# Remainders of two plain weight blocks per slab in the first MLP product: a negative on ScalarE and an adding transfer from GpSimd's queue instead of a subtraction on VectorE

## The chip, the cores and the metric

The kernel runs on one core of a Trainium2 chip. The metric is the device time of one execution in microseconds (us), the median of several runs. One more execution is recorded by the hardware profiler; all durations of single instructions come from that one.

Five engines have instruction streams of their own and meet through semaphores: TensorE (PE; its weight loads are listed as PEld), VectorE (DVE), ScalarE (ACT), GpSimd (POOL) and SyncE (SP). Nearly all transfers are issued by SP. A transfer that adds to its destination is issued here by GpSimd.

## The reference

One decoder block on an input of 2048 rows by 1024 channels: a norm, a combined input projection, two mixers (a short gated convolution and a gated linear recurrence), an output projection with a residual, and then the MLP that this change is in:

```python
h = rmsnorm(x, norm_mlp_g[l])
z = jnp.square(jax.nn.relu(jnp.einsum('bsd,df->bsf', h, w_mlp_in[l])))
x = x + jnp.einsum('bsf,fd->bsd', z, w_mlp_out[l])
return rmsnorm(x, final_norm_g)
```

`w_mlp_in` is 1024 by 4096 in float32. It is called `w1` in the kernel.

## The kernel before

The rows are worked in two pairs of blocks of 512 rows. Each pair runs through mixers, output projection and MLP, so the MLP comes twice. In the profiled execution its first product runs at about 468 to 775 us for the first pair and at about 1485 to 1792 us for the second; its second product (`Down`) follows each time.

**Three passes.** TensorE multiplies operands of type fp32r, a rounded float32. Each float32 operand is split in two: `hi` is its rounded copy, `lo` the remainder. Each product is then three passes, `w_hi*H_hi`, `w_hi*H_lo`, `w_lo*H_hi`, and in the code they come in that order for each quarter of the contraction: the third matmul of a product is the first that reads `w_lo`. The split is `split_into` (its two operations are lines 181 and 182): a copy on ScalarE, then a subtraction on VectorE. `split_new` takes two new tiles for it.

**Slabs and products.** The first product is made in eight slabs of 512 columns of `w1`, one object of the class `Up` each (s = 0 to 7). A slab's weights are four raw blocks of 128 x 1024 elements (512 KB): a11, a12, a21, a22, loaded by SP. A scheme with seven products in place of eight works on them. Two products take a raw block as it came from memory (product 1 takes a11, product 2 takes a12). The others take sums made on VectorE by `sums` (s3, s2, and in place a21 and, at line 833, a12), and product 4 takes a22. `prepare(i)` (lines 835 to 837 with the split) makes the two halves for product i. `multiply` (line 857) issues its 24 matmuls. `drain` takes the results from PSUM (copies `snap` at line 869, a relu and a square at lines 874 and 875, sums at lines 886 to 914) and stores them as `d_z`.

**Order.** The products of a slab come as 1, 2, 6, 5, 7, 3, 4. Slabs 0, 1, 2 do their products 1 and 2 first, then their other five; slabs 3 to 7 follow one after the other. `prepare` is called two products ahead of its `multiply` (`LEAD1 = 2`), `sums` four ahead (`SUMS1 = 4`):

```python
for n in range(-LEAD1, len(seq)):
    m = n + LEAD1
    if prepared <= m < len(seq):
        ups[seq[m][0]].prepare(seq[m][1])
    m = n + SUMS1
    if 0 <= m < len(seq):
        ups[seq[m][0]].sums(seq[m][1])
```

In the first pair's MLP, TensorE keeps the order of the code, and a scheduler puts the instructions of ScalarE, VectorE, GpSimd and SP in order. Between the MLP's own instructions it places those that prepare weights for later stages (the `sum_hi` rows on ScalarE). At the start of the second pair's MLP (`pair_before_mlp`, with the last transposes of the block's rows, line 1742), VectorE's and ScalarE's orders are written out too, and slab 0's products 1 and 2 and slab 1's product 1 are prepared there.

GpSimd does next to nothing: 71 operations in the whole kernel, one transfer among them (the gains `gm`, line 2095). It has no instruction in the two stretches of the first product.

Of the kernel before, what the change touches and what calls it, by code (L numbers as in the profile page):

```python
# [10 lines left out]
F32R = mybir.dt.float32r  # L11
AF = mybir.ActivationFunctionType
ALU = mybir.AluOpType
MUL, ADD, SUB, MAX = ALU.mult, ALU.add, ALU.subtract, ALU.max
# [50 lines left out]
def block_kernel(  # L65
# [15 lines left out]
    nc = tc.nc  # L81
# [30 lines left out]
    def wtile(name, shape, dt=F32):  # L112
        return wp.tile(list(shape), dt, tag="w", name=name)
# [66 lines left out]
    def split_into(hi, lo, src, lo_engine=None):  # L180
        nc.scalar.copy(hi, src)  # L181
        return (lo_engine or V).tensor_tensor(lo, src, hi.bitcast(F32), SUB).ins  # L182
# [32 lines left out]
    def take(nm, ahead=AHEAD, lo_engine=None):  # L215
        u = cursor[0]
        assert units[u][0] == nm, (units[u][0], nm)
        cursor[0] += 1
        for v in range(u + 1, u + ahead + 1):
            load_unit(v)  # L220
        if ahead and not (u + ahead + 1 < len(units) and is_kept(u + ahead + 1)):
            load_unit(u + ahead + 1)
        for v in range(u + 1, u + ahead + 1):
            if v < len(units) and units[v][0] == "oB1":
                with tc.high_priority(SOONER):
                    split_unit(v, lo_engine)
            else:
                split_unit(v, lo_engine)
        if KEEP(u, NU):
            put_by(u, splits[u])  # L230
        return splits.pop(u)
# [249 lines left out]
    with tc.manual_schedule(  # L481
# [9 lines left out]
        w = (his, los)  # L491
# [36 lines left out]
        w = take("g0", ahead=0)  # L528
# [9 lines left out]
        w = take("x1", ahead=0)  # L538
# [254 lines left out]
    def split_new(src, new, nm, lo_engine=None):  # L793
        shape = list(src.shape)
        hi = new(nm + "_hi", shape, F32R)
        lo = new(nm + "_lo", shape, F32R)
        made_at["split"] = split_into(hi, lo, src, lo_engine)
        return hi, lo

    class Up:  # L800


# [6 lines left out]
        def load(self, fs=range(2)):  # L809
            v = w1[:, 512 * self.s : 512 * self.s + 512].rearrange(  # L810
                "(h k p) (f c) -> f h p k c", p=P, h=2, f=2
            )
            for f in fs:
                pair = []
                for h in range(2):
                    r = wtile("w1", (P, 4, 256))
                    nc.sync.dma_start(r, v[f, h])
                    pair.append(r)
                if f == 0:
                    self.a11, self.a12 = pair  # L820
                else:
                    self.a21, self.a22 = pair
# [11 lines left out]

        def prepare(self, i):
            src = {1: "a11", 2: "a12", 6: "s2", 5: "a21", 7: "s3", 3: "a12", 4: "a22"}[i]
            self.ready[i] = split_new(getattr(self, src), wtile, "w")

        def multiply(self, i, H):
            w = self.ready.pop(i)  # L840
# [466 lines left out]
    def prepare_sums():  # L1307
# [23 lines left out]
        for nm in PORDER:  # L1331
            a11, a21, a22 = load(nm, 0, 0), load(nm, 1, 0), load(nm, 1, 1)
            yield
            yield
            s3 = temp("s3", W)
            tt(s3, a11, a21, SUB)
            tt(a21, a21, a22, ADD)
            yield
            a12 = load(nm, 0, 1)
            tt(a11, a21, a11, SUB)  # L1340
            hi = split(s3)
            yield
            put(nm, 7, hi, s3)
            hi = split(a21)
            yield
            put(nm, 5, hi, a21)
            tt(a12, a12, a11, SUB)
            yield
            hi = split(a11)
            yield  # L1350
            put(nm, 6, hi, a11)
            hi = split(a12)
            yield
            put(nm, 3, hi, a12)
            yield
# [4 lines left out]
    def prepare_out_sums():  # L1360
# [25 lines left out]
        for g in range(3):  # L1386
            b12, b11, b22 = load(g, 0, 1), load(g, 0, 0), load(g, 1, 1)
            yield
            yield
            t3 = temp("t3", W)  # L1390
            tt(t3, b22, b12, SUB)
            tt(b12, b12, b11, SUB)
            yield
            b21 = load(g, 1, 0)
            tt(b22, b22, b12, SUB)
            hi = split(t3)
            yield
            put(7, g, hi, t3)
            hi = split(b12)
            yield  # L1400
            put(5, g, hi, b12)
            tt(b21, b21, b22, SUB)
            hi = split(b22)
            yield
            put(6, g, hi, b22)
            hi = split(b21)
            yield
            put(4, g, hi, b21)
# [510 lines left out]
    def pair_before_mlp(b, ups):  # L1919
# [165 lines left out]
        def in_sixth(n, t):  # L2085
            prepare(5, s1, n)
            if n < 3:
                fourth_sum(n)
# [28 lines left out]
        def in_fifth(n, t):  # L2117
            prepare(3, of(0, 1), n)
            square(b, t, 0, True)
# [3 lines left out]
        def in_third(n, t):  # L2123
            prepare(7, of(1, 0), n)
            square(b, t, 1, False)
            scaled(b, t, root(b, t))
            if n == 3:
                raw0.extend(temp("raw0") for _ in range(4))
                turn(xs[TORDER[0]], TORDER[0], raw0, gm)
# [299 lines left out]
```

## Time and profile before

| what | value |
| --- | --- |
| median of 3 runs | 2106.95 us (2106.58 to 2107.22) |
| the profiled execution | 2106.28 us, of which 2104.5 us is the span from the first to the last instruction |
| granted TensorE clock in it | 0.999 of full speed |
| first product, first pair | about 468 to 775 us of the span |
| first product, second pair | about 1485 to 1792 us of the span |
| the split's cast and subtraction of one block | 1.05 us on ScalarE, 1.22 us on VectorE |

In a row of the timeline the first number is the start in us of the span, the second how long the row lasts, then engine, line, operation, output tile, input tiles and their shapes; `x3` joins three instructions that follow each other, and brackets at the end tell how long the engine stood idle before and who released it. In the chain of waits the numbers are start and length of a stretch. A table by stretches of time gives, for each stretch, the busy time of PE, PEld, DVE, ACT and POOL, then the granted clock, the mean busy share of the DMA engines, and GB/s.

### The profile page before, as it was taken

The numbers are of one execution on the slowest core, as the hardware profiler recorded it, in microseconds if no ns is written. First come the engines' busy times: TensorE is split into PE (matmuls) and PEld (weight loads), VectorE is DVE, ScalarE is ACT, GpSimd is POOL, SyncE is SP. The second block draws the span as 40 slices with busy tenths as digits, with TensorE's granted clock in tenths as the row PEclk, the third lists the DMA queues.
The fourth block names the chain that finished last, engine by engine and source line by source line (L and its number), as shares of the span: only waits on it lengthen the run. The fifth ranks groups of instructions, "written<-read, shape, count | busy, mean of one in ns | idle before, by whom it ended". The sixth has DMA issues, their size and how long they took to land.

```text
span 2104.5 us, 25165 instructions
## 1 busy us (share of the span) xinstructions
PE 2096.0 (100%) x9396; PEld 1726.4 (82%) x9396; DVE 1603.7 (76%) x1848; ACT 1104.2 (52%) x1438; POOL 54.8 (3%) x71
## 2 busy tenths in 40 slices
PE   9999999999999999999999999999999999999998
PEld 7888888888888888888888887888888888888887
DVE  6889538858775777999997876785886765887776
ACT  6875447726554554444455888234764333333344
POOL 0110000000000000000000100000000000000000
PEclk9999999999999999999999999999999999999999
DMA  9988889743667778689564656775343355854432
GB/s 340 333 307 326 316 327 352 283 174 111 239 251 255 274 286 333 236 315 338 210 259 169 216 207 230 266 266 208 121 166 134 145 185 208 310 178 155 140 120 81
DMA packets 204762, 492.98 MB, mean 234 GB/s; under 512 B 15840, under 2 KB 80352, under 8 KB 204640
## 3 DMA queue, kind: packets, MB, share of 16 engines
q1 hardware_dynamic: 203040, 486.65, 63.9%
q10 hardware_dynamic: 1568, 4.72, 0.6%
q8 instruction: 74, 1.21, 0.2%
q14 instruction: 48, 0.39, 0.1%
q0 software_dynamic: 32, 0.00, 0.0%
HBM read 324.59 MB, written 166.72 MB: 233 GB/s over the span
## 4 chain that ended last, share of the span: by engine, by line
PE 99%; DVE 1%; ACT 0%; issue 0%; POOL 0%; ACTq 0%; POOLq 0%
PE up L857 42%; PE dn L975 28%; PE po L267 6%; PE ps_g L240 4%; PE wo_x L1889 3%; PE ps_x L240 3%; PE ps_v L240 2%; PE ps_b L240 2%; PE ps_c L240 2%; PE wo_w L1889 2%; PE wo_y L1889 1%; PE tps L1742 1%; PE psri L1498 1%; PE psri L692 1%; PE start_x L518 1%; PE start_x L240 1%
## 5 line engine op out<-in xcount | busy, mean ns | idle before, releaser
L857 PE MATMUL up<-H,w_hi 128*128 128x512 f32 x2576 | 795.0, 390 | 0.0
L857 PEld LDWEIGHTS up<-H,w_hi 128*128 128x128 f32 x2576 | 482.3, 188 | 102.5 <-issue 1.8
L857 PE MATMUL up<-H,w_lo 128*128 128x512 f32 x1288 | 501.5, 389 | 0.0
L975 PE MATMUL dn<-w_hi,z_hi 128*128 128x512 f32 x864 | 336.1, 389 | 0.0
L975 PE MATMUL dn<-w_lo,z_hi 128*128 128x512 f32 x864 | 336.1, 389 | 0.0
L975 PE MATMUL dn<-w_hi,z_lo 128*128 128x512 f32 x864 | 336.1, 389 | 0.0
L857 PEld LDWEIGHTS up<-H,w_lo 128*128 128x128 f32 x1288 | 241.7, 188 | 51.4 <-DVE w_lo L182 0.9
L181 ACT CAST z_hi<-z 128x1024 fp32r<-128x1024 f32 x112 | 118.0, 1053 | 306.3 <-PE dn L975 213.7
L182 DVE TENSOR_TENSOR w_lo<-w,w_hi 128x1024 fp32r<-128x1024 f32 x156 | 190.4, 1222 | 68.1 <-ACT w_hi L181 25.8
L181 ACT CAST w_hi<-w 128x1024 fp32r<-128x1024 f32 x156 | 162.5, 1049 | 131.4 <-PE up L857 52.6
L975 PEld LDWEIGHTS dn<-w_lo,z_hi 128*128 128x128 f32 x864 | 162.2, 188 | 33.9
L975 PEld LDWEIGHTS dn<-w_hi,z_lo 128*128 128x128 f32 x864 | 162.2, 188 | 33.7
L975 PEld LDWEIGHTS dn<-w_hi,z_hi 128*128 128x128 f32 x864 | 162.2, 188 | 33.4
L1007 DVE TENSOR_TENSOR x<-dn,x 128x1024 f32<-128x1024 f32 x108 | 131.1, 1222 | 23.2 <-PE dn L975 23.0
L182 DVE TENSOR_TENSOR z_lo<-z,z_hi 128x1024 fp32r<-128x1024 f32 x112 | 136.7, 1220 | 3.0 <-ACT z_hi L181 3.0
L869 ACT COPY snap<-up 128x1024 f32<-128x1024 f32 x48 | 48.7, 1015 | 73.9 <-PE up L857 73.4
L874 ACT ACTIVATE snap<-snap 128x1024 f32<-128x1024 f32 x33 | 35.1, 1062 | 75.7 <-DVE snap L894 26.5
L182 DVE TENSOR_TENSOR w_lo<-raw,w_hi 128x1024 fp32r<-128x1024 f32 x44 | 53.3, 1221 | 12.1 <-ACT w_hi L181 9.7
L1889 PE MATMUL wo_x<-w_o,y_hi 128*128 128x512 f32 x192 | 59.8, 392 | 0.0
L267 PE MATMUL po<-w_hi,y_hi 128*128 128x512 f32 x192 | 59.6, 393 | 0.0
L267 PE MATMUL po<-w_hi,y_lo 128*128 128x512 f32 x192 | 59.4, 390 | 0.0
L267 PE MATMUL po<-w_lo,y_hi 128*128 128x512 f32 x192 | 59.2, 389 | 0.0
(425 smaller groups left out, 3290.1 us busy)
## 6 DMA issues: line engine op xcount, KB each, us to landing
z<-d_z SPq DMA_DIRECT2D x112, 512.0 KB, 5.9
w<-in_w_mlp_in_dram SPq DMA_DIRECT2D x64, 512.0 KB, 5.9
d_z<-snap SPq DMA_DIRECT2D x64, 512.0 KB, 3.3
w_hi<-d_w SPq DMA_DIRECT2D x55, 512.0 KB, 6.4
w_lo<-d_w SPq DMA_DIRECT2D x55, 512.0 KB, 6.1
d_z<-z SPq DMA_DIRECT2D x48, 512.0 KB, 3.0
w<-in_w_mlp_out_dram SPq DMA_DIRECT2D x48, 512.0 KB, 8.8
d_w<-w_hi SPq DMA_DIRECT2D x40, 512.0 KB, 6.6
```

Source lines behind the costliest of these rows:

```text
L181: nc.scalar.copy(hi, src)
L182: return (lo_engine or V).tensor_tensor(lo, src, hi.bitcast(F32), SUB).ins
L240: nc.tensor.matmul(ps[:, j, lo:hi], ws[k // 4][:, k % 4, j * P : (j + 1) * P], hs[:, k, lo:hi], start=k == 0 and i == 0, stop=k == KD - 1 ...
L267: nc.tensor.matmul(ps[:, half, :], ys[:, j, t * P : (t + 1) * P], ws[j][:, 0, half * 512 : (half + 1) * 512], start=first and i == 0, stop ...
L518: nc.tensor.matmul(start_x[:, j], w[a][k // 4][:, k % 4, j * P : (j + 1) * P], h[c][:, k], start=k == 0 and n == 0, stop=k == KD - 1 and n ...
L692: nc.tensor.matmul(pr_[:, e, :], ws[own, c - gates[2], :], xsrc[own, j, :], start=i == 0, stop=i == 2)
L857: nc.tensor.matmul(ps[:, j, :], ws[:, k, j * P : (j + 1) * P], hs(k), start=i in (1, 2, 5) and k == 0 and n == 0, stop=k == 3 and n == len ...
L869: made_at["snap"] = nc.scalar.copy(t, ps).ins
L874: nc.scalar.activation(t, t, AF.Relu)
L975: nc.tensor.matmul(ps[t // 2][:, t % 2, :], zs[:, p, t * P : (t + 1) * P], ws[:, p, :], start=i in (1, 2, 5) and a == 0 and p == 0 and n == 0,
L1007: V.tensor_add(xt[b, th, dh], ps[th], xt[b, th, dh])
L1889: nc.tensor.matmul(ps[t // 2][:, t % 2, :], ys[:, j, t * P : (t + 1) * P], ws[:, j, :], start=first and n == 1, stop=final and n == 6 * le ...
```

## The change

For products 1 and 2 of slabs 1 to 7 (14 blocks in each of the two MLPs, 28 in all), `lo` is no longer made by VectorE. ScalarE writes the rounded copy `hi` as before, and right behind it a second operation writes the negative of the raw block, rounded in the same way, into `lo`. Then a transfer issued from GpSimd's queue adds the raw block to `lo`, in place: `lo = -round(src) + src`. For product 1 the transfer reads the raw block from memory a second time (`self.raw`, 128 partitions with four runs of 1 KB each); for product 2 it reads the tile a12 (128 runs of 4 KB). Slab 0 and all other products keep the subtraction.

```diff
+    def split_by_queue(src, again, new, nm):
+
+        shape = list(src.shape)
+        hi = new(nm + "_hi", shape, F32R)
+        lo = new(nm + "_lo", shape, F32R)
+        nc.scalar.copy(hi, src)
+        nc.scalar.activation(lo, src, AF.Copy, scale=-1.0)
+        nc.gpsimd.dma_start(lo, again, accum_op=ADD)
+        return hi, lo
+
...
+            self.raw = v[0, 0]
...
         def prepare(self, i):
             src = {1: "a11", 2: "a12", 6: "s2", 5: "a21", 7: "s3", 3: "a12", 4: "a22"}[i]
-            self.ready[i] = split_new(getattr(self, src), wtile, "w")
+            src = getattr(self, src)
+            if i in (1, 2) and self.s > 0:
+                again = self.raw if i == 1 else src
+                self.ready[i] = split_by_queue(src, again, wtile, "w")
+            else:
+                self.ready[i] = split_new(src, wtile, "w")
```

The lines behind it shift by 10 and then by 16: the matmul of line 857 is line 873 after, the copies and relus of lines 869, 874 and 875 are 885, 890 and 891. The new cast is line 805, the negative line 806, the adding transfer line 807.

The next rows show ScalarE before slab 5 of the first pair, as the kernel before has them: the last three rows of slab 4's work, then the casts for slab 4's product 4 (`w_hi_5379`) and for slab 5's products 1 and 2 (`w_hi_5412`, `w_hi_5458`).

```order
L874 ACTIVATE snap_5363<-snap_5363 128x1024
L875 ACTIVATE snap_5363<-snap_5363 128x1024
L181 CAST w_hi_5379<-w1_5094 128x1024
L181 CAST w_hi_5412<-w1_5371 128x1024
L181 CAST w_hi_5458<-w1_5373 128x1024
L874 ACTIVATE snap_5328<-snap_5328 128x1024
L875 ACTIVATE snap_5328<-snap_5328 128x1024
```

The same place after the change, where `w_lo_5421` and `w_lo_5468` are the remainders of slab 5's products 1 and 2.

```order
L890 ACTIVATE snap_5371<-snap_5371 128x1024
L891 ACTIVATE snap_5371<-snap_5371 128x1024
L181 CAST w_hi_5387<-w1_5100 128x1024
L805 CAST w_hi_5420<-w1_5379 128x1024
L806 ACTIVATE w_lo_5421<-w1_5379 128x1024
L805 CAST w_hi_5467<-w1_5381 128x1024
L806 ACTIVATE w_lo_5468<-w1_5381 128x1024
L890 ACTIVATE snap_5336<-snap_5336 128x1024
L891 ACTIVATE snap_5336<-snap_5336 128x1024
```

The casts keep their place; each negative stands directly behind its cast, and the second cast moves back by one operation.

ScalarE before slab 3 of the first pair is another case. After the change it reads as follows (`w_lo_4864` is the remainder of slab 3's product 1).

```order
L181 CAST w_hi_4823<-w1_4506 128x1024
L805 CAST w_hi_4863<-w1_4815 128x1024
L890 ACTIVATE snap_4810<-snap_4810 128x1024
L806 ACTIVATE w_lo_4864<-w1_4815 128x1024
L891 ACTIVATE snap_4810<-snap_4810 128x1024
```

Here the relu of a result tile stands between the cast and its negative.

At the start of the second pair's first product, ScalarE has these rows before the change: casts of activations (`H5`, `H6`), the casts of slab 2's products 1 (`w_hi_12114`) and 2 (`w_hi_12149`), and a copy and a relu of slab 1's results.

```order
L181 CAST H5_11995<-raw0_11555 128x2x128
L181 CAST w_hi_12114<-w1_11986 128x1024
L869 COPY snap_12147<-up_12122 128x1024
L181 CAST H6_11991<-T2_11952 128x2x128
L181 CAST w_hi_12149<-w1_11988 128x1024
L874 ACTIVATE snap_12147<-snap_12147 128x1024
```

After the change the same place reads as follows.

```order
L181 CAST H5_12010<-raw0_11569 128x2x128
L805 CAST w_hi_12130<-w1_12001 128x1024
L806 ACTIVATE w_lo_12131<-w1_12001 128x1024
L181 CAST H6_12006<-T2_11967 128x2x128
L885 COPY snap_12164<-up_12139 128x1024
L805 CAST w_hi_12166<-w1_12003 128x1024
L806 ACTIVATE w_lo_12167<-w1_12003 128x1024
L890 ACTIVATE snap_12164<-snap_12164 128x1024
```

Slab 2's two negatives come in here, and slab 1's two stand some rows earlier in the same stretch, so that four operations have been added to ScalarE by the end of it.

GpSimd after the change, around slabs 4 to 6 of the first pair (before the change these rows aren't there, and the row in front of them is followed by the next stage's copies).

```order
L807 DMA w_lo_5143<-in_w_mlp_in_dram 128x4x256
L807 DMA w_lo_5190<-w1_5096 128x1024
L807 DMA w_lo_5421<-in_w_mlp_in_dram 128x4x256
L807 DMA w_lo_5468<-w1_5381 128x1024
L807 DMA w_lo_5705<-in_w_mlp_in_dram 128x4x256
L807 DMA w_lo_5752<-w1_5658 128x1024
```

The 28 adding transfers stand behind each other in the order of use, with nothing between them inside one MLP.

## The prediction

> **What bounds the kernel now.** I read the profile's page first: busy time by engine, and the chain of work that ended last by engine and by line.
>
> ```profile
> span 2104.5 us, 25165 instructions
> PE 2096.0 (100%) x9396; PEld 1726.4 (82%) x9396; DVE 1603.7 (76%) x1848; ACT 1104.2 (52%) x1438; POOL 54.8 (3%) x71
> PE 99%; DVE 1%; ACT 0%; issue 0%; POOL 0%; ACTq 0%; POOLq 0%
> ```
>
> TensorE is busy all the time and is 99% of the chain. Next, the list of TensorE's waits has one row, and the chain has two stretches of the first product.
>
> ```profile
> PE start_x L486 <- POOL ones_raw L279: 1.1, 1, 1.1
> ```
>
> ```profile
> 480.81 294.05 PE up L857 x1296
> ...
> 1498.39 294.18 PE up L857 x1296
> ```
>
> 1296 matmuls in 294.05 us are 226.9 ns each, with no wait in either stretch; a product of 24 is 5.45 us and a slab of seven 38.1 us. The change takes no matmul away, so what it takes off VectorE cannot shorten these stretches. It can only add waits on TensorE. The third look, the table of busy time by stretch, shows who has time to spare.
>
> ```profile
> 468.00:775.00 307.00, 307.00 (x1363) 254.01 (x1362) 227.99 (x223) 169.89 (x188) 0.00 (x0) 1.00 0.64 233
> 1485.00:1515.00 30.00, 30.00 (x144) 24.75 (x143) 25.79 (x57) 23.82 (x65) 0.00 (x0) 1.00 0.44 158
> 1515.00:1792.00 277.00, 277.00 (x1224) 229.34 (x1223) 187.69 (x161) 116.78 (x115) 0.00 (x0) 1.00 0.45 165
> ```
>
> VectorE is 74% busy in the first MLP's stretch and 68% in the second's long one, and nobody waits for it there. The one crowded place is the start of the second (25.79 and 23.82 of 30 us).
>
> **What is removed and added.** Removed: 28 subtractions on VectorE, 28 x 1.22 = 34 us of busy time, off the path: worth nothing. Added: 28 negatives on ScalarE. The nearest rows are activations of the same shape.
>
> ```profile
> L182 DVE TENSOR_TENSOR w_lo<-w,w_hi 128x1024 fp32r<-128x1024 f32 x156 | 190.4, 1222 | 68.1 <-ACT w_hi L181 25.8
> L874 ACT ACTIVATE snap<-snap 128x1024 f32<-128x1024 f32 x33 | 35.1, 1062 | 75.7 <-DVE snap L894 26.5
> ```
>
> That is 28 x 1.06 = 30 us on ScalarE, which is 55% busy in the first MLP's stretch and 42% in the second's long one: hidden, except where it comes between a cast and its user. Three casts in a row take 2.94 us (row below), so one operation moves what is behind it by 0.95 us.
>
> The chain of a remainder changes its shape. Before: cast, then 1.22 us on VectorE. After: cast, negative, then the transfer, which GpSimd issues when the negative is done. GpSimd has nothing else there. I call L the time from the negative's end to the landing. No row of before shows it. The nearest are these transfers, and the one that GpSimd issued.
>
> ```profile
> w<-in_w_mlp_in_dram SPq DMA_DIRECT2D x64, 512.0 KB, 5.9
> d_z<-snap SPq DMA_DIRECT2D x64, 512.0 KB, 3.3
> prm<-in_rows_t_dram SPq DMA_DIRECT2D x1, 52.0 KB, 2.4
> gm<-in_mlp_g_t_dram POOLq DMA_DIRECT2D x1, 4.0 KB, 4.6
> ```
>
> ```profile
> 1.54 0.67 POOL L2095 DMA_DIRECT2D gm<-in_mlp_g_t_dram  x1
> ```
>
> The load of the same 512 KB takes 5.9 us from SyncE's queue. GpSimd's 4 KB took 4.6 where SyncE's 52 KB took 2.4, so 2.2 us go to GpSimd's queue. L = 5.9 + 2.2 = 8.1, taken as **8**. Lower end: the fastest row of the size, 3.3 us, with nothing added: 3.4. Upper end: the add reads two operands, 2 x 5.9, plus 2.2, plus 2.0 for the rows to be described (128 rows took GpSimd 0.67 us; product 1's transfer has 512, three times 0.67 more): 16.0. I take the load since it is the same block through the same engines at the same load; a spill only reads SBUF.
>
> The Trainium skill's "DMA: Bandwidth & Descriptors", section "Anatomy of one DMA — SWDGE (gpsimd) path", fits 2.0 us plus bytes at 436 GB/s to a transfer from GpSimd: an estimate of 3.2 us for 512 KB. The trace's 5.9 us for the plain load and 4.6 for 4 KB speak against it here; by it the sum below would be 3.7 us instead of 14.6.
>
> **Where L doesn't fit.** For each slab I compare the negative's end with the first matmul that reads `w_lo` in before: the difference is the room. Slab 5, first MLP: ScalarE's three casts (the second is product 1's), then TensorE's first matmuls of product 1.
>
> ```profile
> 652.88 2.94 ACT L181 CAST w_hi<-w 128x1024 fp32r<-128x1024 f32 x3
> ```
>
> ```profile
> 660.36 0.62 PE L857 MATMUL up<-H,w_hi 128*128 128x512 f32 x2
> 660.81 0.39 PE L857 MATMUL up<-H,w_lo 128*128 128x512 f32 x1
> ```
>
> The second cast ends at 652.88 + 0.95 + 1.05 = 654.9, the negative at 655.8: room 5.0, late by L - 5.0. Product 2's negative comes two operations later (1.9 us), its use 5.45 later, so it is covered by the first's wait. Slab 6 is alike: 691.07 gives 694.0, room 5.0.
>
> ```profile
> 691.07 2.93 ACT L181 CAST w_hi<-w 128x1024 fp32r<-128x1024 f32 x3
> ```
>
> ```profile
> 698.99 0.39 PE L857 MATMUL up<-H,w_lo 128*128 128x512 f32 x1
> ```
>
> Slab 3: the casts end earlier, but in the new order a relu stands ahead of the negative, and it waits for VectorE.
>
> ```profile
> 574.60 1.06 ACT L874 ACTIVATE snap<-snap 128x1024 f32<-128x1024 f32 x1 [1.84 <-DVE snap L894]
> ```
>
> ```profile
> 584.48 0.39 PE L857 MATMUL up<-H,w_lo 128*128 128x512 f32 x1
> ```
>
> Negative at 575.6 to 576.6: room 7.9. Slab 2's product 2 (cast at 486.07) has 497.44 - 488.1 = 9.4, and a slip of slab 1 ahead of it is part of that. Slab 4's product 1 (second of two casts, negative done at 611.7) has 10.8. In the new order slab 7's casts stand alike, directly behind slab 6's last; I give it the same.
>
> ```profile
> 486.07 1.06 ACT L181 CAST w_hi<-w 128x1024 fp32r<-128x1024 f32 x1 [0.92 <-PE up L857]
> 608.79 2.00 ACT L181 CAST w_hi<-w 128x1024 fp32r<-128x1024 f32 x2
> ```
>
> ```profile
> 497.44 0.39 PE L857 MATMUL up<-H,w_lo 128*128 128x512 f32 x1
> 622.56 0.39 PE L857 MATMUL up<-H,w_lo 128*128 128x512 f32 x1
> ```
>
> The second MLP's start is the tightest: ScalarE's casts of slab 1's two blocks, then slab 2's first; VectorE's remainder of slab 2's; TensorE's first use of it.
>
> ```profile
> 1494.04 1.04 ACT L181 CAST w_hi<-w 128x1024 fp32r<-128x1024 f32 x1
> 1500.40 1.09 ACT L181 CAST w_hi<-w 128x1024 fp32r<-128x1024 f32 x1
> 1506.95 1.08 ACT L181 CAST w_hi<-w 128x1024 fp32r<-128x1024 f32 x1
> ```
>
> ```profile
> 1508.51 1.22 DVE L182 TENSOR_TENSOR w_lo<-w,w_hi 128x1024 fp32r<-128x1024 f32 x1
> ```
>
> ```profile
> 1509.79 0.50 PE L857 MATMUL up<-H,w_lo 128*128 128x512 f32 x1
> ```
>
> Even before, the remainder was done 0.06 us ahead of its use. With the change the negative ends at 1508.0 + 0.95 = 1509.0 and the transfer is L - 0.8 late; slab 1's two negatives ahead of it on a ScalarE without idle time add up to 1.9. Between L - 0.8 and L + 1.1 I take L + 0.5, since that engine is nearly full. This includes what TensorE has already lost at slab 1: it is the lateness of the last tight use, not a sum over uses. Later in that MLP there is room for any L in question: slab 3's first cast ends at 1579.0 and its use is at 1602.45.
>
> ```profile
> 1577.91 1.05 ACT L181 CAST w_hi<-w 128x1024 fp32r<-128x1024 f32 x1
> ```
>
> ```profile
> 1602.45 0.39 PE L857 MATMUL up<-H,w_lo 128*128 128x512 f32 x1
> ```
>
> One wait is added on VectorE: the in-place sum into a12 may not start before the transfer that reads a12 has landed. Slab 5's stood here.
>
> ```profile
> 663.02 1.22 DVE L833 TENSOR_TENSOR w<-w,w 128x1024 f32<-128x1024 f32 x1
> ```
>
> The transfer lands at 657.7 + 8 = 665.7, so VectorE stands up to 2.7 us with the remainders of products 5 and 3 behind it; TensorE meanwhile is 3 us late itself. I cost it at nothing; uncovered, it would be those 2.7 us twice. The 28 transfers' 14 MB on DMA engines 64% and 45% busy are in L's bounds.
>
> **The sum.** (L + 0.5) + 2(L - 5.0) + (L - 7.9) + (L - 9.4) + 2(L - 10.8), each bracket only where positive. L = 8: 8.5 + 6.0 + 0.1 = **14.6**. L = 3.4: 3.9. L = 5: 5.5. L = 10.5: 25.7. L = 12.5: 39.1. L = 16: 63.6. The profiled execution has 2106.28 us, 1.78 of them around its span; the median of the runs is 2106.95, 0.67 more. The span would go from 2104.5 to 2119.1, the median to **2121.6**. A measurement of this kernel can tell about 0.2%, 4.2 us, from no change.
>
> **The rivals.**
> - Short transfers, the other side. If the adding transfer is as fast as a spill, only the second MLP's start pays. The point is L + 0.5 = 4.2: below L = 3.7 the change can't be told from none (2110.8 at 3.4), from there to L = 5 it costs up to 5.5 (2112.4). For it: the spill's 3.3. Against it: 4.6 us for GpSimd's 4 KB. Chance 0.17, of it 0.08 below 3.7. This is where the page's fit would put it.
> - Long transfers: L from 10.5 to 16, since the add reads its destination too and 512 rows are described by software; then slabs 2, 3, 4 and 7 wait also: 2132.7 to 2170.6. For it: the upper end's terms, and DMA engines 64% busy. Against it: nothing in before adds. Chance 0.18. The Trainium skill's "Collectives: The Full Stack", section "The bandwidth ceiling: the fold count and why AG ≠ RS ≠ AR", says that a reduction runs at half a copy's rate since each chunk needs two source reads; no run here shows it.
> - The granted clock falls after each wait. At L = 8 TensorE stands still for 3 us or more at slabs 5 and 6 and once or twice at the second start. If half a product (12 matmuls) behind a wait runs at half speed, each takes 227 ns longer, 2.7 us a wait: for two such waits 2121.6 + 5.4 = 2127.0, for all four 2132.4. For it: nothing, the clock is 1.00 in all three stretches, which have no waits. Chance 0.12. The Trainium skill's "TensorE: Matmul & The Clock Gate", section "Part 1: The HAM clock gate (the "warmup" mystery)", puts the half clock behind an idle window of about 3.4 us; no run here shows it.
> - VectorE's freed 34 us shorten something. They would have to release a TensorE that waits, and its only wait is 1.1 us at the program's start. Chance 0.02, about 2100.
>
> **How the numbers follow.** The forecast (L from 5 to 10.5, 2112.4 to 2132.7) has 0.51. Faster by over 0.2%: 0.02. Within: 0.08. Slower: 0.51 + 0.12 + 0.18 + 0.09 = 0.90. The range: at the low end 2106.95 + 4.2 = 2111.2, which leaves out 0.10; at the high end L = 12.5, 2146, which leaves out about half of the long case, 0.09.
>
> **What would show it.** Right: waits of TensorE for a GpSimd transfer into `w_lo` of about 3 us at slabs 5 and 6 of the first MLP and about 8.5 in all at the second's start, none at its slabs 3 to 7; 8 us from issue to landing for the 28 transfers; the same matmul time between. Wrong: a landing time under 4 or over 10.5; waits for VectorE's sum into a12 (the cover is gone); matmuls of over 227 ns behind a wait (the clock); or TensorE without such waits.

## The result, and the profile after

The changed kernel takes 2124.38 us (median of 4 runs, 2123.95 to 2125.22) where the kernel before took 2106.80 beside it (4 runs): 1.0084 times as long, interval 1.0066 to 1.0101. That is 17.6 us more. The profiled execution took 2123.95 us with a span of 2122.2, 17.7 more than before.

The page of the changed kernel: span, busy time by engine, and the chain that ended last.

```profile
span 2122.2 us, 25296 instructions
PE 2100.6 (99%) x9396; PEld 1727.8 (81%) x9396; DVE 1573.7 (74%) x1820; ACT 1130.7 (53%) x1466; POOL 85.8 (4%) x99
PE 84%; DVE 4%; issue 3%; DMA 2%; ACT 1%; SPq 0%; DVEq 0%; POOLq 0%; POOL 0%; ACTq 0%
```

VectorE lost 30 us of busy time (the prediction had 34) and ScalarE gained 26.5 (30), and the chain, 99% TensorE before, is 84% TensorE now. The list of TensorE's waits had one row before. Now it has these.

```profile
PE up L873 <- DMA w_lo<-in_w_mlp_in_dram: 10.3, 5, 2.7
PE start_x L486 <- POOL ones_raw L279: 1.1, 1, 1.1
PE up L873 <- ACT r L1765: 1.1, 1, 1.1
PE start_x L518 <- ACT w_hi L501: 0.8, 1, 0.8
PE dn L991 <- DVE w_lo L182: 0.8, 1, 0.8
PE po L267 <- DVE ys_B L626: 0.2, 1, 0.2
```

Five waits for adding transfers, all for product 1's. Three stand in the first MLP, at slabs 3, 5 and 6: the first matmul that reads `w_lo`, with TensorE's idle time ahead of it in brackets (up to 0.35 us less than what is lost, as the matmul in front runs on for a while).

```profile
588.85 0.50 PE L873 MATMUL up<-H,w_lo 128*128 128x512 f32 x1 [1.87 <-DMA w_lo<-in_w_mlp_in_dram]
666.87 0.50 PE L873 MATMUL up<-H,w_lo 128*128 128x512 f32 x1 [1.34 <-DMA w_lo<-in_w_mlp_in_dram]
707.82 0.50 PE L873 MATMUL up<-H,w_lo 128*128 128x512 f32 x1 [2.58 <-DMA w_lo<-in_w_mlp_in_dram]
```

The issues of these three on GpSimd, each about 0.4 us behind the end of its negative.

```profile
579.33 1.29 POOL L807 DMA_DIRECT2D w_lo<-in_w_mlp_in_dram  x1 [87.11 <-DVE s L839]
660.77 1.32 POOL L807 DMA_DIRECT2D w_lo<-in_w_mlp_in_dram  x1 [39.21 <-ACT w_lo L806]
700.48 1.30 POOL L807 DMA_DIRECT2D w_lo<-in_w_mlp_in_dram  x1 [36.99 <-ACT w_lo L806]
```

TensorE goes on 0.05 us after a landing, so issue to landing took 9.5, 6.05 and 7.3 us here. With the 0.4 us ahead of the issue, L was 9.9, 6.5 and 7.7.

The other two waits, and one for ScalarE, are at the second MLP's start.

```profile
1508.42 0.73 PE L873 MATMUL up<-H,w_hi 128*128 128x512 f32 x2 [1.09 <-ACT r L1765]
1511.82 0.56 PE L873 MATMUL up<-H,w_lo 128*128 128x512 f32 x1 [2.67 <-DMA w_lo<-in_w_mlp_in_dram]
1512.17 1.06 PE L873 MATMUL up<-H,w_hi 128*128 128x512 f32 x2
...
1526.41 0.50 PE L873 MATMUL up<-H,w_lo 128*128 128x512 f32 x1 [1.82 <-DMA w_lo<-in_w_mlp_in_dram]
```

Both kernels issue the same 9396 matmuls in the same order, so the start of each in before can be subtracted from the start of the same one here. What is added to that difference at a place is what the place cost:

| place | us added |
| --- | --- |
| ahead of slab 3 of the first MLP (2.0 of it ahead of the MLP: start of the program, output projection) | 2.3 |
| first MLP, slab 3 | 2.2 |
| first MLP, slab 5 | 1.7 |
| first MLP, slab 6 | 2.8 |
| second MLP's start (slabs 1 and 2) | 7.6 |
| second MLP, second product | 1.1 |
| sum | 17.7 |

14.3 of the 17.7 us stand at the four places that the prediction named. 3.4 us stand outside them. (The expectations below go by 17.5 and 3.2.)

### The profile page after: what moved, and what is told of

It is laid out like the page before. It is cut to its first block, busy times and chain, and to the rows that moved or that the text cites. A ratio compares the mean times of both kernels' runs of the same rounds, so it can differ in the third digit from the quotient of the medians.

```text
span 2122.2 us, 25296 instructions
## 1 busy us (share of the span) xinstructions
PE 2100.6 (99%) x9396; PEld 1727.8 (81%) x9396; DVE 1573.7 (74%) x1820; ACT 1130.7 (53%) x1466; POOL 85.8 (4%) x99
## 4 chain that ended last, share of the span: by engine, by line
PE 84%; DVE 4%; issue 3%; DMA 2%; ACT 1%; SPq 0%; DVEq 0%; POOLq 0%; POOL 0%; ACTq 0%
PE up L873 37%; PE dn L991 26%; PE po L267 5%; PE wo_x L1905 3%; PE ps_g L240 2%; PE ps_x L240 2%; PE wo_w L1905 2%; DMA w_lo<-in_w_mlp_in_dram 1%; PE ps_v L240 1%; PE ps_b L240 1%; PE ps_c L240 1%; PE wo_y L1905 1%; PE psri L1514 1%; PE tps L1758 1%; PE dn L1010 1%
## 5 line engine op out<-in xcount | busy, mean ns | idle before, releaser
L181 ACT CAST w_hi<-w 128x1024 fp32r<-128x1024 f32 x128 | 133.8, 1049 | 109.8 <-PE up L873 32.3
L182 DVE TENSOR_TENSOR w_lo<-w,w_hi 128x1024 fp32r<-128x1024 f32 x128 | 156.1, 1221 | 47.0 <-PE dn L991 20.5
L910 DVE TENSOR_TENSOR snap<-up,snap 128x1024 f32<-128x1024 f32 x16 | 19.6, 1222 | 63.3 <-PE up L873 63.3
L182 DVE TENSOR_TENSOR w_lo<-raw,w_hi 128x1024 fp32r<-128x1024 f32 x44 | 53.3, 1220 | 11.2 <-ACT w_hi L181 10.8
```

## The experiments

The theory was lateness: TensorE loses, at each place by itself, the time by which a transfer's landing comes after the first use. One rival was traffic: the added bytes slow all transfers, and the loss goes with their number. The other was ScalarE: the negatives themselves push what comes after them. All kernels are timed beside the kernel before (2107.23 us in the first group of four, 2107.13 in the second, 2106.71 in the third). The table has the us added at each place in the profile of each run, against the first profile of the kernel before; the run that made each transfer twice, with 112 us spread over the slabs, is left out.

| kernel | time, us | ahead | slab 3 | 5 | 6 | 7 | second start | second product |
| --- | --- | --- | --- | --- | --- | --- | --- | --- |
| the change | 2124.38 | 2.3 | 2.2 | 1.7 | 2.8 | 0 | 7.6 | 1.1 |
| before, again | 2107.19 | 1.2 | 0 | 0 | 0 | 0 | -0.1 | 0 |
| product 1 only | 2124.54 | 0.9 | 2.3 | 1.8 | 1.7 | 4.0 | 6.7 | 0.3 |
| product 2 only | 2112.87 | 0.1 | 0 | -0.2 | 0 | 0 | 5.9 | 0.8 |
| tight places undone | 2112.69 | 0.1 | 0 | 0 | 0 | 6.6 | 0 | 1.1 |
| copy, no add | 2115.40 | 0.3 | 0 | 0 | 1.6 | 0 | 5.6 | 0.9 |
| add by VectorE | 2111.73 | 0.7 | 0 | 0 | 0 | 0 | 4.8 | 1.4 |
| both from the tile | 2114.63 | 0.3 | 0 | 0 | 1.5 | 0 | 5.7 | 0 |
| second MLP, slabs 3 to 7 | 2107.70 | 0.2 | 0 | 0 | 0 | 0 | 0 | 1.7 |
| first MLP only | 2115.80 | 0.7 | 2.3 | 1.9 | 2.7 | 0 | 0 | 0.7 |
| second MLP, slabs 1 and 2 | 2114.67 | 0.8 | 0 | 0 | 0 | 0 | 7.5 | 0 |

**The kernel before, again.** No edit.

> The kernel before once more, with a new profile. In the changed kernel 14.3 us of TensorE's 17.5 us delay stand in front of adding transfers; 2.3 us more were lost before the first product began and 0.9 us in the second product of the second pair. If those 3.2 us are differences between executions, this run shows delays of about 1 us at the same two places against the first profile of the same kernel, and a time of 2106 to 2108 us. If they are the change's doing, both places are within 0.2 us of the first profile.

2107.19 us, 0.9999 of before (0.9990 to 1.0008). Its list of TensorE's waits has a second row, at the program's start.

```profile
PE start_x L486 <- POOL ones_raw L279: 1.1, 1, 1.1
PE start_x L518 <- ACT h_hi L497: 1.1, 1, 1.1
```

1.2 us at the first place differ between two executions of one kernel, so of the 2.3 us about half and perhaps all is no work of the change. At the second place this run shows nothing; that is taken up below.

**Product 1 only.**

```diff
-            if i in (1, 2) and self.s > 0:
+            if i == 1 and self.s > 0:
```

> Only product 1 (raw block read again from memory) is changed, 14 blocks. Theory A, lateness: TensorE waits only where a transfer lands after the use, each wait being L less the room of that place, with L as the changed kernel showed it from the negative's end: 6.5 us from memory, 9.9 at slab 3, 7.7 at slab 6. Then the first MLP still loses about 2.1 + 1.7 + 2.8 = 6.6 us, the second's start 6.6 - 0.8 + 0.95 = 6.7 (one negative ahead instead of two): 13.3, or 2120 us, up to 3 more outside. Theory B, traffic: the added bytes slow the other transfers, so the loss follows the number of transfers: half of 17.6, about 2115.6. Theory C, ScalarE: the loss follows the negatives: half, about 2115.6, and without waits for transfers.

2124.54 us, 1.0082 (1.0068 to 1.0096): half the transfers and half the negatives cost as much as all of them. Traffic and ScalarE alone would both have given 2115.6; both fall as the whole cause. At the second start 6.7 us were forecast and 6.7 came: slab 2's transfer landed at 1527.21, and its first use followed at 1527.26. The 4.0 us by which lateness missed the total are at slab 7, where the transfer was issued later and landed after 9.67 us (the chain of waits there): 2.1 us are the wait, the rest is mostly matmuls at half the granted clock behind it.

```profile
736.36 9.67 DMA w_lo<-in_w_mlp_in_dram
```

**Product 2 only.**

```diff
-            if i in (1, 2) and self.s > 0:
+            if i == 2 and self.s > 0:
```

> Only product 2 (raw block read from its tile) is changed, 14 blocks. Theory A, lateness: at slabs 5 and 6 the room of product 2 is 9.5 us (its use is 5.45 later) and L was 7.3 and 8.9 there: no wait in the first MLP. At the second's start the second block of slab 1 is used 1504.25 in before, its negative would end at 1502.4, L is 4.9 undisturbed: 3.1 us late, up to 4.7 if the matmuls behind that wait run slowly: 2110 to 2112 us. Theory B, traffic: half of 17.6: 2115.6. Theory C, ScalarE: half: 2115.6.

2112.87 us, 1.0024 (1.0014 to 1.0033). No wait in the first MLP, and one in the second, 3.3 us late as worked out (3.1). What came on top is in the rows behind it and in the granted clock, the third figure from the end of the rows by stretch.

```profile
1507.58 0.79 PE L873 MATMUL up<-H,w_lo 128*128 128x512 f32 x1 [3.21 <-DMA w_lo<-w]
1508.17 1.05 PE L873 MATMUL up<-H,w_hi 128*128 128x512 f32 x2
1509.02 0.63 PE L873 MATMUL up<-H,w_lo 128*128 128x512 f32 x1
```

```profile
1507.50:1510.50 3.00, 2.92 (x7) 2.34 (x8) 3.00 (x6) 3.00 (x6) 0.00 (x0) 0.50 0.29 112
1510.50:1513.50 3.00, 3.00 (x9) 2.32 (x8) 1.55 (x3) 1.50 (x2) 0.87 (x1) 0.53 0.00 0
1513.50:1517.00 3.50, 3.50 (x17) 2.83 (x16) 1.41 (x2) 0.15 (x1) 0.00 (x0) 1.00 0.76 150
```

Behind the wait the clock is 0.50 for some 6 us, and the matmuls start 0.43 us apart instead of 0.227: 2.8 us more, which with the 3.3 make 6.1 (5.9 in the table, since 0.2 is made up right behind). The ten executions of this kernel bear it out: the two with a mean granted clock of 0.999 took 2109.9 and 2110.1 us, the eight with 0.997 or 0.998 took 2111.2 to 2114.3.

**The tight places undone** (slabs 3, 5, 6 of the first MLP, 1 and 2 of the second).

```diff
-            if i in (1, 2) and self.s > 0:
+            if i in (1, 2) and self.s in ((1, 2, 4, 7) if self.by_act else (3, 4, 5, 6, 7)):
```

> The change is undone at the five tight places (slabs 3, 5, 6 of the first MLP, slabs 1 and 2 of the second); 18 of the 28 blocks keep it. Theory A, lateness: no wait of TensorE for an adding transfer, 2107 to 2108 us, plus whatever of the 3.2 us outside is the change's. Theory B, traffic: 18/28 of 17.6, 11.3 us: 2118. Theory C, ScalarE: 18/28 as well, less where ScalarE has idle time; at least 2109.

2112.69 us, 1.0025 (1.0015 to 1.0035). The five places are at nothing, but slab 7, which had room 10.8 in the changed kernel, now waits. ScalarE there, then TensorE:

```profile
728.38 1.06 ACT L890 ACTIVATE snap<-snap 128x1024 f32<-128x1024 f32 x1 [3.92 <-DVE snap L910]
729.35 1.03 ACT L805 CAST w_hi<-w 128x1024 fp32r<-128x1024 f32 x1
730.29 1.05 ACT L891 ACTIVATE snap<-snap 128x1024 f32<-128x1024 f32 x1
731.24 1.04 ACT L806 ACTIVATE w_lo<-w 128x1024 fp32r<-128x1024 f32 x1
```

```profile
740.84 0.80 PE L873 MATMUL up<-H,w_lo 128*128 128x512 f32 x1 [3.50 <-DMA w_lo<-in_w_mlp_in_dram]
741.43 1.05 PE L873 MATMUL up<-H,w_hi 128*128 128x512 f32 x2
```

The scheduler has put the cast behind a relu that waits for VectorE, and the square in front of the negative. The negative is done at 732.3, the use was at 737.15: room 4.9, L 8.5, late 3.7, and 2.8 for the clock. (This profile is of an execution of 2114.0 us, 1.3 over the median.) The forecast for this kernel was wrong, since it took the place as fixed; lateness itself gives the number once the order is read.

**A copy without the add** (`lo` is then the raw block itself).

```diff
-        nc.gpsimd.dma_start(lo, again, accum_op=ADD)
+        nc.gpsimd.dma_start(lo, again)
```

> The same 28 transfers without the add: GpSimd's queue copies the raw block over the negative, so lo is wrong by the whole block and only the time counts. In the changed kernel an adding transfer lands 6.0 to 6.2 us after its issue from memory and 4.4 from a tile when it is undisturbed. If the add is the dear part (a second read), a copy lands after about 4 and 3 us, L falls by 2, and the loss with it: no wait at slabs 5 and 6, about 5.7 at the second's start: about 2114 us. If the queue and its descriptors are the dear part, the landing times stay within 0.5 us and so does the run's time: 2121 to 2125.

2115.40 us, 1.0043 (1.0028 to 1.0058), near the 2114 of a dear add. The medians from issue to landing and their spread over both sources, first of the changed kernel, then of this one:

```profile
w_lo<-in_w_mlp_in_dram POOLq DMA_DIRECT2D x14, 512.0 KB, 6.1
w_lo<-w POOLq DMA_DIRECT2D x14, 512.0 KB, 5.6
...
DMA to landing us min/median/max: 4.4/6.1/9.5
```

```profile
w_lo<-in_w_mlp_in_dram POOLq DMA_DIRECT2D x14, 512.0 KB, 4.2
w_lo<-w POOLq DMA_DIRECT2D x14, 512.0 KB, 2.9
...
DMA to landing us min/median/max: 2.8/4.0/6.9
```

SyncE's loads of `w1`'s blocks in before, the same size:

```profile
DMA to landing us min/median/max: 3.6/5.9/7.9
```

The add is the dear part, not the queue. A copy from memory on GpSimd's queue that nothing disturbs lands after 3.9 to 4.2 us, SyncE's fastest load of a block after 3.6. That fastest one is the only one of the 64 during which no other transfer of SyncE's was under way; with five or more others under way the loads took 5.3 to 7.9 us. So the median of 5.9 is the price of a load in company. At slab 6 both are disturbed: the copy landed after 6.2 us, the add after 7.3.

**The add by VectorE** (ScalarE's negatives stay, no transfer).

```diff
-        nc.gpsimd.dma_start(lo, again, accum_op=ADD)
+        V.tensor_tensor(lo, src, lo.bitcast(F32), ADD)
```

> ScalarE's 28 negatives stay, and VectorE adds the raw block in place of the transfer: nothing is left out, and no GpSimd transfer is left. Theory A, lateness: the chain is cast, 0.95 us, 1.2 us; room 5 us holds it at slabs 5, 6 and 3. At the second's start two negatives push slab 2's first remainder by 1.9 us with its own 0.95 us more: 2 to 3 us, no more: 2109 to 2110.5. Theory C, ScalarE: as the changed kernel, 2120 or more. If the small waits in the second pair's second product (0.3 to 1.1 us in every changed kernel so far) come from the transfers, they are gone here.

2111.73 us, 1.0022 (1.0012 to 1.0031); 4.8 us at the second start.

```profile
PE up L873 <- DVE w_lo L807: 2.3, 1, 2.3
PE start_x L486 <- POOL ones_raw L279: 1.1, 1, 1.1
PE dn L991 <- DVE w_lo L182: 0.9, 1, 0.9
PE up L873 <- ACT r L1765: 0.7, 1, 0.7
```

3.3 us are waits for what ScalarE does later (0.9) and for the remainder (2.35); 1.5 are slow matmuls behind. The profile is of an execution of 2113.51 us, 1.8 over the median; the five executions with a mean granted clock of 0.999 took 2110.0 to 2111.2 us, the five with 0.998 took 2112.2 to 2114.4. So ScalarE's negatives have a price of their own, at that one place, and not in the first MLP, where nothing was added. The wait in the second product is here without any transfer of the change.

**Each transfer twice.**

```diff
-        nc.scalar.activation(lo, src, AF.Copy, scale=-1.0)
+        nc.scalar.activation(lo, src, AF.Copy, scale=-2.0)
         nc.gpsimd.dma_start(lo, again, accum_op=ADD)
+        nc.gpsimd.dma_start(lo, again, accum_op=ADD)
```

> Each transfer is made twice, one after the other (the negative with scale -2, then the block added twice; the remainder is rounded once more on its way). L from memory becomes about 6.1 + 0.4 + 6.1 + 0.3 = 13. Theory A, lateness, with the rooms of the prediction: second's start 13 + 1.1 = 14; slabs 5 and 6, 8 each; slab 3, 5 to 8; slab 2, 3.6; slabs 4 and 7, 2.2 each; 43 to 46, and if matmuls behind each wait of 3 us run at half speed for about 2.8 us, three or four times 2.8 more: 2150 to 2162 us. Theory B, traffic: twice the bytes, twice the loss: 2142, spread over all slabs.

2222.04 us, 1.0545 (1.0529 to 1.0561), far over both forecasts.

```profile
PE up L874 <- DMA w_lo<-in_w_mlp_in_dram: 68.9, 9, 12.9
PE up L874 <- ACT snap L886: 9.3, 3, 3.8
```

The waits for transfers are at the places forecast and at slab 1, and at slab 5 the size is near: L was 14.8 against a room of 5, and the landing was 9.8 us late. But at slabs 3, 4, 6 and 7 the transfers, those of products 1 and 2 under way at the same time, took up to 10 us each: L was 17 to 21. Slow matmuls behind these waits come on top, 1.8 to 3.2 us each in the first MLP. And three waits are new, for ScalarE's copies. ScalarE waits at such times for VectorE's in-place sum into a12 (line 845):

```profile
ACT w_hi L181 <- DVE w L845: 85.1, 9, 14.1
```

That sum has to wait for the transfer that reads a12. The cover of VectorE's added wait is gone once L is twice as long; this was priced at nothing in the changed kernel, and there it holds.

**Both from the tile.**

```diff
-                again = self.raw if i == 1 else src
+                again = src
```

> Product 1's transfer too reads the raw block from its tile instead of memory: no byte is read twice from memory, and every L falls from 6.5 to about 4.9 us. Theory A, lateness: slabs 5 and 6 lose 0 to 1 us each, slab 3 nothing unless its transfer is disturbed, the second's start 4.9 + 1.1 = 6.0: 7 in all, 2114 us. If VectorE's in-place sum over the tile of product 1 (it makes the operand of product 6) now waits for the transfer and that is not covered, 2 us more at each of slabs 3 to 7 of the first MLP: 2122 or more.

2114.63 us, 1.0036 (1.0023 to 1.0049), as lateness had it.

```profile
w_lo<-w POOLq DMA_DIRECT2D x28, 512.0 KB, 5.0
```

The time is 10.1 us nearer to before than the changed kernel's. By place, 7 us of that are at slabs 3 and 5 (now nothing), slab 6 (1.5) and the second start (5.7); the other 3 are the ones outside these places. VectorE's in-place sum over product 1's tile (s2 is made in a11's tile) waits too now, 29.4 us in all, without a wait on TensorE.

**Only the second MLP's slabs 3 to 7.**

```diff
-            if i in (1, 2) and self.s > 0:
+            if i in (1, 2) and self.s > 2 and not self.by_act:
```

> Only slabs 3 to 7 of the second MLP keep the change, 10 blocks, where the use comes over 18 us after the negative. Lateness: no wait for a transfer, the time of before, 2107 to 2108 us. Traffic: 10/28 of 17.6, 6.3 us: 2113.

2107.70 us, 1.0003 (0.9994 to 1.0012): no difference that can be told, and no wait for a transfer.

```profile
PE start_x L486 <- POOL ones_raw L279: 1.1, 1, 1.1
PE dn L991 <- DVE w_lo L182: 0.9, 1, 0.9
```

Ten adding transfers, 5 MB more on the DMA engines, cost nothing that can be told where there is room. No gain comes with them either.

**The first MLP only, and the second's start only.**

```diff
-            if i in (1, 2) and self.s > 0:
+            if i in (1, 2) and self.s > 0 and self.by_act:
```

```diff
-            if i in (1, 2) and self.s > 0:
+            if i in (1, 2) and self.s in (1, 2) and not self.by_act:
```

> The change in the first MLP only, 14 blocks; ScalarE's order there is the one of the changed kernel. Lateness: 2 us each at slabs 3, 5 and 6, 6.5 in all as in the changed kernel, slab 7 up to 2 more if its transfer is disturbed as in the run with memory only: 2113 to 2116 us. Traffic would give half of 17.6 as well, 2116; then the loss is not in waits for the transfers.

> The change at slabs 1 and 2 of the second MLP only, four blocks of 28. Lateness: what the changed kernel lost there, L + 1.1 with L = 6.6, 7.7 us, plus 0.3 to 1.3 in the second product: 2115 us, nearly half of the whole loss. Traffic: 4/28 of 17.6, 2.5 us: 2109.5. ScalarE's part is the same four negatives as in the run with VectorE's add, which lost 4.8 there with a slow clock behind its wait.

2115.80 us, 1.0043 (1.0030 to 1.0057), and 2114.67 us, 1.0038 (1.0024 to 1.0051): 9.1 and 8.0 us more, 17.1 together beside the whole change's 17.6. By place, without what stands outside, the slabs lose 6.9 and 7.5, 14.4 beside 14.3. The two parts add up, and four of the 28 blocks bring nearly half of the loss. Lateness had 2113 to 2116 and 2115.

```profile
PE up L873 <- DMA w_lo<-in_w_mlp_in_dram: 6.1, 3, 2.5
```

```profile
PE up L873 <- DMA w_lo<-in_w_mlp_in_dram: 3.3, 2, 2.7
```

## Why the prediction was right, and where it wasn't

**The mechanism.** The loss stands where it was put, behind product 1's transfers at slabs 3, 5 and 6 and at the second start, and the parts alone give the parts of the sum. That 14.6 was forecast and 14.3 came there is in part luck: places and rooms were right, the sizes were off both ways. The forecast of 2121.6 us is 2.8 below the 2124.38 measured, less than the 3.4 that stand outside the sum. Slabs 3 to 7 of the second MLP cost nothing, and VectorE's freed time was worth nothing: the run that gave up ten subtractions at no cost was no faster.

**The rooms** held. In the changed kernel slab 5 had 5.0 us from the negative's end to the use at the delay so far (forecast 5.0), slab 6 5.0 (5.0) and slab 3 7.9 (7.9).

**L** was the mis-sized term, and its working was wrong. One L of 8.1 was made of a load, 5.9, and 2.2 for GpSimd's queue, with nothing for the add. Measured, L is 6.5 undisturbed from memory (4.8 from a tile), 7.7 at slab 6 and 9.9 at slab 3. The load was taken too long (5.9 is a load in company, 3.6 one alone, and the copy takes 3.95), the queue too dear (2.2, where the undisturbed copies take 0.3 to 0.6 us more than SyncE's load alone), and the add costs 1.6 to 2.1 us (4.45 against 2.85 from a tile, 6.05 against 3.95 from memory, by the landings that lie together at the low end of each kind). The 0.4 us between the negative's end and the issue were left out as well. So slab 5 lost 1.7 instead of 3.0 and slab 3 2.2 instead of 0.1: sizes off both ways that nearly cancel (6.7 against 6.1 for the first MLP). In the stretches of those transfers (580, 661 and 700 us) the DMA engines' busy share was:

```profile
579.33:588.80 9.47, 7.65 (x34) 6.01 (x32) 7.61 (x7) 8.42 (x9) 2.16 (x2) 1.00 0.88 232
660.77:666.82 6.05, 4.75 (x21) 3.57 (x19) 5.91 (x7) 5.79 (x7) 2.21 (x2) 1.00 0.73 116
700.48:707.77 7.29, 4.76 (x21) 3.59 (x20) 6.35 (x7) 7.24 (x8) 2.19 (x2) 1.00 1.00 238
```

The late ones fall in the busy stretches (0.88 and 1.00, at twice the GB/s). That SyncE's transfers hold them up is argued from this, not shown by a run. Product 2's adding transfer, which runs beside product 1's, is not the cause at slab 3: with product 1's alone the landing took 9.66 us there. At slab 6 it took 6.14 us without product 2's and 7.29 with it, so there it may have a part.

The page that spoke for short transfers, the Trainium skill's "DMA: Bandwidth & Descriptors", section "Anatomy of one DMA — SWDGE (gpsimd) path", gives an estimate of 3.2 us for this size. For the copies it lies between the measured 2.85 and 3.95; for the adding transfer it is 1.25 and 2.85 us too short. The rival of short transfers, as fast as a spill (3.3), fails with the 6.05 us from memory, on which the terms that counted rest. The Trainium skill's "Collectives: The Full Stack", section "The bandwidth ceiling: the fold count and why AG ≠ RS ≠ AR", has a reduction at half a copy's rate for its second read; here the whole time from issue to landing is 1.5 times the copy's, and no run parts the rate from what is fixed in it.

**The second start** was forecast at L + 0.5 with L = 8, 8.5 us, and cost 7.6. The form was L + 1.1, the upper bound: ScalarE's cast of slab 2's block moved from 1506.95 to 1517.73, 10.8 us, of which TensorE was 8.9 late already; the other 1.9 are slab 1's two negatives in full.

```profile
1517.73 1.08 ACT L805 CAST w_hi<-w 128x1024 fp32r<-128x1024 f32 x1
1518.68 1.08 ACT L806 ACTIVATE w_lo<-w 128x1024 fp32r<-128x1024 f32 x1
```

With L = 6.6 (landing at 1526.36) that makes 7.7. It also shows why the sum takes the last lateness and not all of them.

**The clock** was a rival at 0.12, and it is real. In the changed kernel it falls once:

```profile
1508.00:1511.80 3.80, 0.73 (x2) 0.30 (x2) 3.70 (x9) 3.80 (x10) 0.00 (x0) 1.00 0.92 155
1511.80:1515.60 3.80, 3.78 (x10) 3.00 (x11) 2.10 (x6) 3.80 (x10) 0.90 (x1) 0.55 0.68 136
```

The 1.7 us lost there cost nothing in the end, since the next wait is for ScalarE's chain, which had no idle time and ended when it did; TensorE only came nearer to it. Where no such wait followed it cost its full price: 2.8 us with product 2 only and with the tight places undone, about 1.5 at slab 7 with product 1 only and with the add by VectorE. The prediction had 2.7 us a wait, behind all waits of 3 us; it comes behind some waits and not behind others, as the last section has it.

**VectorE's added wait** is there (6.7 us over five of the 16 sums into a12) and covered, as forecast; the run with each transfer twice shows the cover giving way.

**Outside the sum.** Of the 3.4 us, the 2.3 ahead of slab 3 vary from 0.1 to 2.3 over the runs, 1.2 in a second profile of the kernel before; about half of it is seen without the change, the rest stays open. The 0 to 1.8 us in the second product are TensorE's wait for VectorE's remainder behind a refill of `z`. They stand in nine of the eleven profiles with the change or a part of it, also in the one without any adding transfer, and in neither of the two of the kernel before. Whether the change has a part in them stays open; no run was made on it.

## What to carry to other kernels

Where one engine is busy without a gap, taking work off another engine is worth nothing, and each lengthened chain is weighed by its room: from its last input's end to its first use, in the order that the scheduler has made now, since a scheduler makes a loose place tight without a word. Price a new kind of transfer by one run of it alone (copy and add apart, memory and tile apart), not by adding up rows of other transfers. Keep the one place that had a margin of 0.06 us out of such a change first: four of 28 blocks made nearly half of this loss.

## What the runs showed of the hardware that was not expected

- An adding transfer of 512 KB takes 1.5 times as long as the copy from issue to landing (6.05 against 3.95 us from memory, 4.45 against 2.85 from a tile), and from GpSimd's queue an undisturbed copy from memory takes 3.9 to 4.2 us where SyncE's fastest load of such a block takes 3.6.
- Behind some waits the granted clock is 0.50 and the matmuls start 0.43 us apart instead of 0.227. The low clock lasted 6.8 us where TensorE had waited 3.2 us (product 2 only), 3.5 (the tight places undone), 2.9 and 2.7 (second start, with product 1 only and with slabs 1 and 2 only), and 3.4 us behind waits of 2.1 (slab 7, product 1 only), 2.3 (add by VectorE), 2.35 (both from the tile) and 2.7 (the changed kernel). Behind the waits of 1.3 to 2.0 us at slabs 3 and 5, of 2.5 and 2.6 at slab 6 and of 2.4 at slab 2 (copy, no add) it stayed at 1.00. The Trainium skill's "TensorE: Matmul & The Clock Gate", section "Part 1: The HAM clock gate (the "warmup" mystery)", puts the half clock behind an idle window of about 3.4 us that runs freely. The two lengths, 3.4 and 6.8 us, agree with steps of such a window. The waits do not: 2.1 us were enough here, so on what it takes to lose the clock the measurement decides, and why 2.1 us do it and 2.6 do not stays open.
